# Float32 down products, without parts, in three of seven blocks of the wide experts

## The chip, the cores and the metric

The kernel runs on one core of a Trainium2 chip. The metric is device time in microseconds (us), the median of several executions; lower is better. TensorE is called PE here (its weight loads PEld), VectorE DVE, ScalarE ACT, GpSimd POOL and SyncE SP, as in the profile.

## The reference, cut to what matters

A two-layer trunk on 256 tokens of width 1024. Layer 0 is a retention mixer and a dense SwiGLU, layer 1 a pooling mixer and a top-2-of-8 expert SwiGLU. The change lies in the experts:

```python
def _swiglu(h, w_gate, w_up, w_down):
    return (jax.nn.silu(h @ w_gate) * (h @ w_up)) @ w_down

def expert_block(args):
    xblk, e = args
    return _swiglu(xblk, w_gate[e], w_up[e], w_down[e])
```

An expert has three matrices: gate and up, 1024 x 3584 each, and down, 3584 x 1024. All is float32, and so is the output.

## The kernel before, in words

**Precision by parts.** A float32 weight tile is not multiplied as it is loaded. `split` (L113) makes two tiles of type float32r from it: ACT copies it to the high part `w_hi`, and DVE subtracts that from the tile, which leaves the low part `w_lo`. A product of two float32 numbers is then three float32r matmuls (`mm3`: high x high, high x low, low x high), L156 to L158.

**Weights.** `weights` (L136) loads a 128x4096 piece in two tiles of 128x2048 (1 MB each) called `raw`, and splits each. The loads are issued by SP alone, in the order of the program, into a ring of buffers; twelve of them stay in use through the whole expert stage (six `raw`, four `e8`, `cb` and `T_l`), and some others for a few uses at its beginning. `w_hi` and `w_lo` have three buffers of 2048 columns each (`N_SPL`). A `raw` buffer is free again when DVE has written its `w_lo`; the buffers of the parts are free when PE has used them.

**The experts** come in blocks of 512 of the 3584 hidden columns, seven (`NJ`) for each of eight experts, 56 in all. Each block needs a gate, an up and a down piece: six loads, six splits. The three fullest experts after expert 0 are **wide**: they take 128 tokens, and their products are `mm3`, 48 matmuls of 128x512 for gate and up, 24 for down. The others are **narrow**: they take 64 tokens, and the high and low parts of the tokens stand side by side as the 128 stationary columns, so that `mm2` (L738, L739) does with two matmuls what `mm3` does with three: 32 for gate and up, 16 for down, and the halves are added by small matmuls with `fold` (L774). `BLOCKS` sets the order: the seven blocks of expert 0, then seven times the pattern wide, narrow, wide, narrow, wide, narrow, narrow.

**One iteration** of the main loop (L865) does, for block i, the gate products (`pg`), the up products (`pu`), and then the down products of block i-2 (`down_of`). Between them stand small steps: for a wide block `hidden` (ACT: Silu of `pg` into `sg`; DVE: `moe_h` = `pu` times `sg`) and, an iteration later, `moe_T`, which turns the hidden block by four transposes and splits it into `dT`; for a narrow block ACT copies `g_out` and `u_out`, PE folds them, and ACT and DVE make `sg_n`, `h_n` and `dT`. `prepare` and `combine` gather the tokens of the next expert and give back the sums of the last one. `advance` takes the piece that was loaded last and issues the loads and splits of the next. `behind_next` (L823) puts the small steps that it encloses behind the first half of the splits of the piece in `coming`; ACT and DVE run their instructions in the order of the program, so this says where on these engines the small steps stand.

Of the kernel before, what the change touches and what calls it, by code (L numbers as in the profile page):

```python
# [13 lines left out]
AF = mybir.ActivationFunctionType  # L14
# [5 lines left out]
P = 128  # L20
# [11 lines left out]
NJ = DFE // 512  # L32
# [18 lines left out]
WIDE = tuple(0 < p <= N_WIDE for p in range(NE))  # L51

_wide = iter([(p, j) for p in range(1, N_WIDE + 1) for j in range(NJ)])
_narrow = iter([(p, j) for p in range(N_WIDE + 1, NE) for j in range(NJ)])
BLOCKS = [(0, j) for j in range(NJ)] + [next(_wide if t % 7 in (0, 2, 4) else _narrow) for t in range(7 * NJ)]
assert len(set(BLOCKS)) == NE * NJ and BLOCKS[-1] == (NE - 1, NJ - 1)
ALWAYS = math.inf

# [6 lines left out]
def trunk(ctx, tc, x, cols, c_row, const, ada_0, ada, w_0, w_in, w_out, f_gu, f_dn, pool_w, m_g, m_u, m_d, out):  # L65
    nc = tc.nc
# [6 lines left out]
    def bank():  # L73
        return psA.tile([P, 512], F, tag="a", name="bank")

    def tbank():
        return psT.tile([P, 512], F, tag="t", name="tbank")

    def buf(tag, shape, bufs=1, dt=F, name=None):
        return act.tile([P] + shape, dt, tag=tag, name=name or tag, bufs=bufs)  # L80

    def w2(shape, name, dt=F):
        return buf("w2", shape, 4, dt, name)
# [23 lines left out]
    for h in range(2):  # L107
        ps = tbank()
# [3 lines left out]
    def split(hi, lo, src):  # L112
        return nc.scalar.activation(hi, src, AF.Copy), nc.vector.tensor_sub(lo, src, hi.bitcast(F))  # L113

    @contextmanager
    def behind(*instructions):

        with ExitStack() as s:
            for i in instructions:
                s.enter_context(tc.issue_after(i.ins))  # L120
            yield
# [4 lines left out]
    def load(src, in_halves=False):  # L126
        tag, bufs, uses = ring.popleft()
        if uses > 1:
            ring.append((tag, bufs, uses - 1))
        t = buf(tag, [2048], bufs, name="raw")  # L130
        n = 1024 if in_halves else 2048
        for c in range(0, 2048, n):
            nc.sync.dma_start(t[:, c:c + n], src[:, c:c + n])
        return t

    def weights(src, step=2048, held=((), (), (), ()), in_halves=False):  # L136

        parts, splits = [], []
        for h in range(0, src.shape[1], 2048):
            t = load(src[:, h:h + 2048], in_halves)  # L140
            hi = buf("w_hi", [2048], N_SPL, R)
            lo = buf("w_lo", [2048], N_SPL, R)
            for c in range(0, 2048, step):
                strip = slice(c, c + step)
                with behind(*held[len(splits)]):
                    splits.append(split(hi[:, strip], lo[:, strip], t[:, strip]))
            parts.append((hi, lo))

        def at(c, n=512):
            hi, lo = parts[c // 2048]  # L150
            return hi[:, c % 2048:c % 2048 + n], lo[:, c % 2048:c % 2048 + n]
        at.splits = splits
        return at

    def mm3(ps, xh, xl, wh, wl, start, stop):
# [91 lines left out]
    def transpose4(src):  # L247
        ps = tbank()
        for i in range(4):
            nc.tensor.transpose(ps[:, i * P:(i + 1) * P], src[:, i * P:(i + 1) * P], ident)  # L250
        return ps
# [14 lines left out]
    for b in range(TB):  # L266
        for g in range(0, KD, 4):
            ps = transpose4(xn[:, b, g * P:(g + 4) * P])
# [3 lines left out]
    first = [[tbank() for _ in range(TB)]] + [[bank() for _ in range(TB)] for _ in range(3)]  # L272
    for k in range(KD):
# [5 lines left out]
        at = weights(w_0[k], 1024, held=((), h_k))  # L279
# [90 lines left out]
    for i, f in enumerate(W_REST):  # L370
        at = weights(w_in[i])
# [11 lines left out]
    for h in range(NH):  # L383
        yT = st[f"yT{h}"]
        at = weights(w_out[h])
        last = h == NH - 1
# [16 lines left out]
    for b in range(TB):  # L403
# [9 lines left out]
        for g in range(0, KD, 4):  # L413
            ps = transpose4(xn[:, b, g * P:(g + 4) * P])
# [14 lines left out]
    def gu_block(j, hd_before):  # L429
        at = weights(f_gu[j], **{} if j else dict(step=1024, held=(early, early, late, late)))  # L430
        hd = w2([TB, 256], "ffn_h")
        pss = [bank() for _ in range(TB)]
        th = None
        steps = [(b, k) for b in range(TB) for k in range(KD)] if j == 0 else [(b, k) for k in range(KD) for b in range(TB)]
        for i, (b, k) in enumerate(steps):
            if i == 8 and j:
                th = ffn_T(hd_before)
            wh, wl = at(512 * k)
            mm3(pss[b], hh[:, k, tok(b)], hl[:, k, tok(b)], wh, wl, k == 0, k == KD - 1)
        for b in range(TB):  # L440
            sg = w2([256], "sg")
            nc.scalar.activation(sg, pss[b][:, 0:256], AF.Silu)
            nc.vector.tensor_mul(hd[:, b], pss[b][:, 256:512], sg)
        return hd, th

    def down_weights(j):
        return weights(f_dn[:, 2048 * j:2048 * (j + 1)])
# [6 lines left out]
    hd = None  # L454
    for j in range(NFB):
        hd, th = gu_block(j, hd)
        if 0 < j < NFB - 1:
            at = down_weights(j - 1)
# [14 lines left out]
        if j == 9:  # L473
# [6 lines left out]
            ps = tbank()  # L480
            for k in range(KD):
                nc.tensor.matmul(ps[:, 0:NE], s_m[:, k:k + 1].to_broadcast([P, P]), rt0[:, k],
                                 start=(k == 0), stop=(k == KD - 1))
# [3 lines left out]
    last = [(NFB - 2, down_weights(NFB - 2), th)]  # L487
# [37 lines left out]
    for b in range(TB):  # L525
        pooled = [bank() for _ in range(2)]
        for g in range(0, KD, 4):
            ps = transpose4(xn[:, b, g * P:(g + 4) * P])
# [6 lines left out]
        for n in range(2):  # L535
            ps = bank()
# [6 lines left out]
        for n in range(2):  # L543
            band(pooled[n], n, slice(b * P, (b + 1) * P), hw[:, b], b == 0, True)
            c = slice(512 * n, 512 * (n + 1))
# [6 lines left out]
    for b in range(TB):  # L552
        rs.append(normed(xn, b)[2])
        ps = tbank()
# [4 lines left out]
        ps = tbank()  # L559
# [22 lines left out]
    def sources():  # L582

        def rows(a, i):
            p, j = BLOCKS[i]
            if p == 0:
                return a[j * P:(j + 1) * P, :]
            if expert[p] is None:
                expert[p] = nc.values_load(place_i[0:1, p - 1:p], engines=[SP], min_val=1, max_val=NE - 1,
                                           skip_runtime_bounds_check_because="a permutation of 1 to 7")  # L590
            return a[ds((expert[p] * NJ + j) * P, P), :]

        for i in range(n_blocks + 2):
            if i < n_blocks:
                yield rows(m_g, i)
                yield rows(m_u, i)
            if i > 1:
                yield rows(m_d, i - 2)

    srcs = sources()  # L600


# [3 lines left out]
        ring.insert(place, tuple(spare))  # L606
    ring.extendleft(reversed(once))
    with behind(chain_end):
        coming = weights(next(srcs), 1024)

    ps = tbank()
    wh, _ = coming(0)
# [4 lines left out]
    ps = tbank()  # L617
# [137 lines left out]
        nc.vector.tensor_mul(hd, pu, sg)  # L755
        return hd

    def moe_T(hd):
        ps = transpose4(hd)
        th = buf("dT", [2, 4, P], 2, R, name="dT")  # L760
        split(th[:, 0], th[:, 1], ps.rearrange("p (c t) -> p c t", c=4))
        return th
# [6 lines left out]
    def fold_T(gu):  # L769

        ps = tbank().rearrange("p (g c t) -> p g c t", g=2, c=4)
        for i, a in enumerate(gu):
            for c in range(4):
                nc.tensor.matmul(ps[:, i, c], a[:, c * P:(c + 1) * P], fold, start=True, stop=True)  # L774
        sg = w2([4, HALF], "sg_n")
        nc.scalar.activation(sg, ps[:, 0], AF.Silu)
        hd = w2([4, HALF], "h_n")
        nc.vector.tensor_mul(hd, ps[:, 1], sg)
        th = buf("dT", [4, 2, HALF], 2, R, name="dT")
        split(th[:, :, 0], th[:, :, 1], hd)  # L780
        return th

    def down(at, th, ye, first, last, narrow=False):
        for c in range(4):
            for n in range(2):
                wh, wl = at(1024 * c + 512 * n)
                if narrow:
                    mm2(ye[n], th[:, c], wh, wl, first and c == 0, last and c == 3)
                else:
                    mm3(ye[n], th[:, 0, c], th[:, 1, c], wh, wl, first and c == 0, last and c == 3)  # L790
# [31 lines left out]

    def behind_next():  # L823

        return behind(*coming.splits[len(coming.splits) // 2]) if coming else nullcontext()

    def advance():
        nonlocal coming
        at, src = coming, next(srcs, None)
        coming = None if src is None else weights(src)  # L830
        return at

    steps, first_steps = [], []
# [3 lines left out]
            (first_steps or steps).pop(0)()  # L837

    def turned_of(i, parts):
        return moe_T(parts) if WIDE[BLOCKS[i][0]] else fold_T(parts)  # L840

    def picked(a, placed, p):
        return pick(a, 0) if p == 0 else pick(placed, p - 1)
# [1 line left out]
    outs, ths = {}, {}  # L845

    def down_of(i):
        p, j = BLOCKS[i]
        if j == 0:
            outs[p] = [bank(), bank()]  # L850
        down(advance(), ths.pop(i), outs[p], j == 0, j == NJ - 1, not WIDE[p])
        if j == NJ - 1 and p < NE - 1:
            while steps:
                steps.pop(0)()
            steps.extend(combine(outs[p], ready[p][1], picked(gate, gate_p, p), g2_row))
            steps.pop(0)()
# [7 lines left out]
    mid = None  # L864
    for i, (p, j) in enumerate(BLOCKS):  # L865
        wide = WIDE[p]
# [29 lines left out]
    last = coming  # L896
# [21 lines left out]
    with tc.If(most > 0):  # L918
        slot2 = cst.tile([P, TB, NE], F, name="slot2")
        nc.vector.tensor_sub(slot2, slot, room.rearrange("p (o e) -> p o e", o=1).to_broadcast([P, TB, NE]))  # L920
        with tc.For_i(0, NE, 1) as e:
# [10 lines left out]
            ye = [bank(), bank()]  # L932
            for j in range(NJ):
                at = ds((e * NJ + j) * P, P)
                hd = hidden(up(weights(m_g[at, :]), xe), up(weights(m_u[at, :]), xe))
# [87 lines left out]
```

## Time and profile before

| | us |
|---|---|
| median of 3 runs | 1374.58 (1373.06 to 1376.11) |
| the profiled execution, its own time | 1376.74 |
| its span, first to last instruction | 1375.0 |
| PE busy in the span | 1315.1 (96%) |
| PEld busy | 1052.5 (77%) |
| DVE busy | 1215.2 (88%) |
| ACT busy | 978.2 (71%) |
| DMA of the span | 477.30 MB, mean 347 GB/s |

A row of the view of groups gives line, engine, operation, output<-inputs and count, then the busy time and the mean of one. In the view in order of time a row gives start, duration, engine, line and operation, and in brackets how long the engine was idle before it and which instruction ended that. A PE matmul's duration contains its way through the array, in which the next one already runs: what it costs a stream is the distance from its start to the next start.

### The profile page before, as it was taken

What the parts mean: (1) busy time and instruction counts of PE and PEld (TensorE: products, weight loads), DVE (VectorE), ACT (ScalarE), POOL (GpSimd) and SP (SyncE); (2) the same over time, 40 slices, a digit from 0 to 9 for tenths busy, and PEclk for the clock granted to TensorE, in tenths of its full rate; (3) what the DMA queues carried; (4) which work ended last, traced back from release to release, by engine and by line L of the source; (5) the groups of instructions that cost most, each with busy time, mean ns of one, the idle gap of its engine ahead of it and who ended that gap; (6) DMA issues with size and microseconds to landing.
All of it is one profiled execution on the core that took longest, in us unless ns stands there. A gap on an engine that the chain in (4) does not pass through costs nothing.

```text
span 1375.0 us, 16794 instructions
## 1 busy us (share of the span) xinstructions
PE 1315.1 (96%) x6136; PEld 1052.5 (77%) x6136; DVE 1215.2 (88%) x1121; ACT 978.2 (71%) x942; POOL 0.2 (0%) x4
## 2 busy tenths in 40 slices
PE   7999998999999899999999999999999999999995
PEld 5787876888887777778778877788778777777874
DVE  7889867998867698999989999989998989999997
ACT  6655465444445698878878887878878878788884
POOL 0000000000000000000000000000000000000000
PEclk9999999999999899999999999999999999999998
DMA  9987885998786599999999999999999999999960
GB/s 384 380 278 260 324 287 207 338 378 362 297 333 238 209 427 344 369 364 424 419 377 401 424 334 334 412 356 426 412 357 409 360 334 401 404 367 418 424 279 33
DMA packets 66474, 477.30 MB, mean 347 GB/s; under 512 B 7377, under 2 KB 7761, under 8 KB 8658
## 3 DMA queue, kind: packets, MB, share of 16 engines
q1 hardware_dynamic: 66386, 476.17, 88.3%
q8 instruction: 50, 0.82, 0.2%
q14 instruction: 38, 0.31, 0.1%
HBM read 475.10 MB, written 1.05 MB: 346 GB/s over the span
## 4 chain that ended last, share of the span: by engine, by line
PE 70%; DVE 16%; ACT 6%; issue 4%; DMA 3%; DVEq 0%; SPq 0%; ACTq 0%
PE bank L157 15%; PE bank L158 15%; PE bank L156 14%; DVE w_lo L113 12%; PE bank L739 8%; PE bank L738 7%; PE tbank L774 3%; ACT w_hi L113 3%; DMA raw<-in_m_d_dram 2%; PE tbank L720 2%; PE tbank L250 1%; DVE raw L167 1%; ACT xe_f L240 1%; DMA raw<-in_m_u_dram 1%; DVE dT L113 1%
## 5 line engine op out<-in xcount | busy, mean ns | idle before, releaser
L113 DVE TENSOR_TENSOR w_lo<-raw,w_hi 128x2048 fp32r<-128x2048 f32 (+1 forms) x413 | 907.1, 2225 | 82.5 <-ACT w_hi L113 78.4
L113 ACT ACTIVATE w_hi<-raw 128x2048 fp32r<-128x2048 f32 (+1 forms) x413 | 763.8, 1868 | 199.1 <-PE bank L158 142.3
L739 PE MATMUL bank<-w_lo,xe_n 128*128 128x512 f32 x560 | 230.7, 412 | 12.7 <-DVE w_lo L113 9.6
L738 PE MATMUL bank<-w_hi,xe_n 128*128 128x512 f32 x560 | 221.1, 396 | 2.0 <-DVE xe_n L113 2.0
L739 PEld LDWEIGHTS bank<-w_lo,xe_n 128*128 128x128 f32 x560 | 105.8, 189 | 57.5 <-DVE w_lo L113 38.0
L156 PE MATMUL bank<-w_hi,T_h 128*128 128x512 f32 x352 | 140.9, 401 | 3.0 <-ACT T_h L113 3.0
L157 PE MATMUL bank<-w_lo,T_h 128*128 128x512 f32 x352 | 138.5, 393 | 2.4 <-DVE w_lo L113 2.4
L158 PE MATMUL bank<-w_hi,T_l 128*128 128x512 f32 x352 | 138.8, 394 | 1.7 <-DVE T_l L113 1.7
L157 PE MATMUL bank<-w_lo,xe 128*128 128x512 f32 x336 | 132.5, 394 | 0.9 <-DVE w_lo L113 0.9
L156 PE MATMUL bank<-w_hi,xe 128*128 128x512 f32 x336 | 131.6, 392 | 0.0
L158 PE MATMUL bank<-w_hi,xe 128*128 128x512 f32 x336 | 130.9, 390 | 0.0
L738 PEld LDWEIGHTS bank<-w_hi,xe_n 128*128 128x128 f32 x560 | 106.0, 189 | 22.1 <-DVE xe_n L113 2.1
L167 DVE SCALAR_TENSOR_TENSOR raw<-raw,cb 128x1024 f32<-128x1024 f32 x96 | 114.4, 1218 | 1.7 <-DMA raw<-in_ada_dram 1.7
L739 PE MATMUL bank<-w_lo,dT 128*128 128x512 f32 x280 | 104.4, 411 | 7.2 <-DVE w_lo L113 6.7
L738 PE MATMUL bank<-w_hi,dT 128*128 128x512 f32 x280 | 100.1, 394 | 1.7 <-DVE dT L113 1.7
L157 PE MATMUL bank<-w_lo,dT 128*128 128x512 f32 x256 | 100.8, 394 | 0.7 <-DVE w_lo L113 0.7
L158 PE MATMUL bank<-w_hi,dT 128*128 128x512 f32 x256 | 99.8, 390 | 0.0
L156 PE MATMUL bank<-w_hi,dT 128*128 128x512 f32 x256 | 94.2, 389 | 0.0
L156 PEld LDWEIGHTS bank<-w_hi,T_h 128*128 128x128 f32 x352 | 66.6, 189 | 17.7 <-ACT T_h L113 4.3
L158 PEld LDWEIGHTS bank<-w_hi,T_l 128*128 128x128 f32 x352 | 66.5, 189 | 17.1 <-DVE T_l L113 3.2
L157 PEld LDWEIGHTS bank<-w_lo,T_h 128*128 128x128 f32 x352 | 66.6, 189 | 16.4 <-DVE w_lo L113 2.8
L157 PEld LDWEIGHTS bank<-w_lo,xe 128*128 128x128 f32 x336 | 63.1, 188 | 16.3 <-DVE w_lo L113 3.8
(227 smaller groups left out, 1430.5 us busy)
## 6 DMA issues: line engine op xcount, KB each, us to landing
raw<-in_m_g_dram SPq DMA_DIRECT2D x112, 1024.0 KB, 7.5
raw<-in_m_u_dram SPq DMA_DIRECT2D x112, 1024.0 KB, 7.6
raw<-in_m_d_dram SPq DMA_DIRECT2D x112, 1024.0 KB, 7.3
raw<-in_ada_dram SPq DMA_DIRECT2D x48, 1024.0 KB, 7.2
raw<-in_f_gu_dram SPq DMA_DIRECT2D x22, 1024.0 KB, 6.9
raw<-in_w_in_dram SPq DMA_DIRECT2D x16, 1024.0 KB, 5.2
raw<-in_f_dn_dram SPq DMA_DIRECT2D x11, 1024.0 KB, 7.2
raw<-in_w_dram SPq DMA_DIRECT2D x8, 1024.0 KB, 8.7
```

Source lines behind the costliest of these rows:

```text
L113: return nc.scalar.activation(hi, src, AF.Copy), nc.vector.tensor_sub(lo, src, hi.bitcast(F))
L156: nc.tensor.matmul(ps, xh, wh, start=start, stop=False)
L157: nc.tensor.matmul(ps, xh, wl, start=False, stop=False)
L158: nc.tensor.matmul(ps, xl, wh, start=False, stop=stop)
L167: nc.vector.scalar_tensor_tensor(s, s, 1.0, cb, op0=ALU.mult, op1=ALU.mult, accum_out=mod[:, m:m + 1])
L240: nc.scalar.activation(out, ps, AF.Identity, scale=a[:, k:k + 1], bias=s[:, k:k + 1])
L250: nc.tensor.transpose(ps[:, i * P:(i + 1) * P], src[:, i * P:(i + 1) * P], ident)
L720: nc.tensor.matmul(ps[:, i * ns:(i + 1) * ns], xn[:, b, c], oh[:, b, 0:ns], start=(b == 0), stop=(b == TB - 1))
L738: nc.tensor.matmul(ps, x, wh, start=start, stop=False)
L739: nc.tensor.matmul(ps, x, wl, start=False, stop=stop)
L774: nc.tensor.matmul(ps[:, i, c], a[:, c * P:(c + 1) * P], fold, start=True, stop=True)
```

## The change

In the blocks 1, 3 and 5 (of 0 to 6) of each wide expert, nine blocks in all, the down piece is loaded and not split. `moe_T` then makes one float32 tile (`dT_f`, by one ACT copy) in place of the two parts, and `down` does eight float32 matmuls of 128x512 on the `raw` tiles in place of 24 float32r ones. `behind_next` has nothing to stand behind where such a piece is in `coming`.

```diff
+WHOLE = {(p, j) for p, j in BLOCKS if WIDE[p] and j % 2}
...
+    def whole_weights(src):
+
+        parts = [load(src[:, h:h + 2048]) for h in range(0, src.shape[1], 2048)]
+
+        def at(c, n=512):
+            return parts[c // 2048][:, c % 2048:c % 2048 + n]
+        at.splits = []
         return at
...
-                yield rows(m_g, i)
-                yield rows(m_u, i)
+                yield weights, rows(m_g, i)
+                yield weights, rows(m_u, i)
             if i > 1:
-                yield rows(m_d, i - 2)
+                yield whole_weights if BLOCKS[i - 2] in WHOLE else weights, rows(m_d, i - 2)
...
-    def moe_T(hd):
+    def moe_T(hd, whole=False):
         ps = transpose4(hd)
+        if whole:
+            t = buf("dT", [4, P], 2, name="dT_f")
+            nc.scalar.activation(t, ps.rearrange("p (c t) -> p c t", c=4), AF.Copy)
+            return t
...
-    def down(at, th, ye, first, last, narrow=False):
+    def down(at, th, ye, first, last, narrow=False, whole=False):
         for c in range(4):
             for n in range(2):
+                if whole:
+                    nc.tensor.matmul(ye[n], th[:, c], at(1024 * c + 512 * n), start=first and c == 0, stop=last and c == 3)
+                    continue
...
-        return behind(*coming.splits[len(coming.splits) // 2]) if coming else nullcontext()
+        return behind(*coming.splits[len(coming.splits) // 2]) if coming and coming.splits else nullcontext()
```

**What moves on DVE.** The place is the iteration of a wide block after a narrow one, whose down piece is a whole one (the fourth wide place of the second wide expert). Before, from the `moe_h` of the wide block ahead of it:

```order
578 L755 TENSOR_TENSOR moe_h<-bank,sg 128x512
579 L113 TENSOR_TENSOR w_lo<-raw,w_hi 128x2048 x4
580 L113 TENSOR_TENSOR dT<-tbank,dT 128x512
581 L113 TENSOR_TENSOR w_lo<-raw,w_hi 128x2048 x6
582 L778 TENSOR_TENSOR h_n<-tbank,sg_n 128x256
583 L113 TENSOR_TENSOR w_lo<-raw,w_hi 128x2048
584 L113 TENSOR_TENSOR dT<-h_n,dT 128x4x64
585 L113 TENSOR_TENSOR w_lo<-raw,w_hi 128x2048
586 L755 TENSOR_TENSOR moe_h<-bank,sg 128x512
587 L113 TENSOR_TENSOR w_lo<-raw,w_hi 128x2048 x4
```

Now:

```order
564 L766 TENSOR_TENSOR moe_h<-bank,sg 128x512
565 L115 TENSOR_TENSOR w_lo<-raw,w_hi 128x2048 x10
566 L793 TENSOR_TENSOR h_n<-tbank,sg_n 128x256
567 L115 TENSOR_TENSOR dT<-h_n,dT 128x4x64
568 L766 TENSOR_TENSOR moe_h<-bank,sg 128x512
569 L115 TENSOR_TENSOR w_lo<-raw,w_hi 128x2048 x4
```

The subtraction for `dT` of the whole block and the two splits of its down piece are gone; `moe_h`, which needs the up products of this iteration, now follows `dT` directly.

**What moves on ACT.** The place is the last narrow block of the first pattern that has a whole down piece in its iteration. Before:

```order
361 L113 ACTIVATE w_hi<-raw 128x2048 x4
362 L766 ACTIVATE g_out<-bank 128x512
363 L776 ACTIVATE sg_n<-tbank 128x256
364 L113 ACTIVATE w_hi<-raw 128x2048
365 L113 ACTIVATE dT<-h_n 128x4x64
366 L113 ACTIVATE w_hi<-raw 128x2048
367 L766 ACTIVATE u_out<-bank 128x512
368 L113 ACTIVATE w_hi<-raw 128x2048 x4
```

Now:

```order
357 L115 ACTIVATE w_hi<-raw 128x2048 x4
358 L781 ACTIVATE g_out<-bank 128x512
359 L791 ACTIVATE sg_n<-tbank 128x256
360 L115 ACTIVATE dT<-h_n 128x4x64
361 L781 ACTIVATE u_out<-bank 128x512
362 L115 ACTIVATE w_hi<-raw 128x2048 x4
```

The two copies of the down piece are gone, and `u_out`, which needs the up products, stands ahead of the four copies of the next gate and up pieces with only `dT` before it. On SP nothing moves.

## Rows read from the trace of the kernel before

**Rows 1.** The page: busy time of each engine over the span.
```profile
PE 1315.1 (96%) x6136; PEld 1052.5 (77%) x6136; DVE 1215.2 (88%) x1121; ACT 978.2 (71%) x942; POOL 0.2 (0%) x4
```

**Rows 2.** Busy by stretch: expert stage; a narrow and a wide iteration (with PEclk, DMA share, GB/s).
```profile
475.00:1345.00 870.00, 845.69 (x4011) 678.09 (x4010) 814.75 (x509) 720.20 (x591) 0.00 (x0) 1.00 0.96 381
946.90:960.30 13.40, 13.39 (x65) 10.54 (x64) 12.98 (x8) 12.55 (x10) 0.00 (x0) 1.00 1.01 426
960.30:977.10 16.80, 16.80 (x78) 13.91 (x77) 15.84 (x10) 12.82 (x10) 0.00 (x0) 1.00 1.01 426
```

**Rows 3.** The page: the chain of waits over the span, by engine.
```profile
PE 70%; DVE 16%; ACT 6%; issue 4%; DMA 3%; DVEq 0%; SPq 0%; ACTq 0%
```

**Rows 4.** In order of time: PE through a wide block's down products, 24 matmuls.
```profile
970.51 0.62 PE L156 MATMUL bank<-w_hi,dT 128*128 128x512 f32 x2
...
975.73 0.39 PE L158 MATMUL bank<-w_hi,dT 128*128 128x512 f32 x1
975.96 0.39 PE L738 MATMUL bank<-w_hi,xe_n 128*128 128x512 f32 x1
```

**Rows 5.** In order of time, PE: two float32 matmuls of 128x512 (L340) and the next.
```profile
81.57 1.88 PE L340 MATMUL bank<-a,sT 128*128 128x512 f32 x4
83.29 1.02 PE L342 MATMUL bank<-a,sT 128*128 128x512 f32 x2
```

**Rows 6.** Float32 matmuls at the kernel's end (L807): all of them; weight loads in time.
```profile
L807 PE MATMUL tbank<-yp,ohT x8: 592/592/697, 1359.7 to 1363.2; 128*128 128x512 f32 x8
...
1360.26 0.19 PEld L807 LDWEIGHTS tbank<-yp,ohT 128*128 128x128 f32 x1 [0.24 <-issue]
1360.69 0.19 PEld L807 LDWEIGHTS tbank<-yp,ohT 128*128 128x128 f32 x1 [0.24 <-issue]
```

**Rows 7.** Instructions by tile, 475 to 1345 us: ns min/median/max; loads from issue to landing.
```profile
L113 DVE TENSOR_TENSOR w_lo<-raw,w_hi x326: 2278/2286/2296, 473.0 to 1342.7; 128x2048 fp32r<-128x2048 f32 x163
L113 ACT ACTIVATE w_hi<-raw x325: 1892/1919/1993, 477.1 to 1342.9; 128x2048 fp32r<-128x2048 f32 x163
L113 DVE TENSOR_TENSOR dT<-tbank,dT x21: 682/684/687, 580.8 to 1323.7; 128x512 fp32r<-128x512 f32 x21
DMA to landing us min/median/max: 4.7/7.4/10.2
```

**Rows 8.** Waits of PE and of PEld, 475 to 1345 us: total, times, longest.
```profile
PE bank L739 <- DVE w_lo L113: 16.3, 29, 1.4
PE bank L157 <- DVE w_lo L113: 1.6, 5, 0.5
PEld bank L739 <- DVE w_lo L113: 57.1, 98, 1.9
PEld bank L157 <- DVE w_lo L113: 5.8, 14, 1.0
```

**Rows 9.** Waits of PEld: first and last of nine stretches, 623.2 to 668.8 and 1301.5 to 1331.7.
```profile
PEld bank L739 <- DVE w_lo L113: 2.1, 5, 0.5
...
PEld bank L739 <- DVE w_lo L113: 1.1, 3, 0.4
```

**Rows 10.** In order of time, ACT in the wide iteration of rows 2.
```profile
962.55 1.92 ACT L113 ACTIVATE w_hi<-raw 128x2048 fp32r<-128x2048 f32 x1 [1.12 <-PE bank L158]
965.27 1.92 ACT L113 ACTIVATE w_hi<-raw 128x2048 fp32r<-128x2048 f32 x1 [0.53 <-PE bank L158]
```

**Rows 11.** In order of time, ACT, DVE and PE in the narrow iteration after it.
```profile
980.28 0.60 ACT L766 ACTIVATE g_out<-bank 128x512 f32<-128x512 f32 x1
980.77 0.59 ACT L113 ACTIVATE dT<-tbank 128x512 fp32r<-128x512 f32 x1
981.25 3.73 ACT L113 ACTIVATE w_hi<-raw 128x2048 fp32r<-128x2048 f32 x2
...
983.21 6.70 DVE L113 TENSOR_TENSOR w_lo<-raw,w_hi 128x2048 fp32r<-128x2048 f32 x3
...
985.55 0.73 PE L739 MATMUL bank<-w_lo,dT 128*128 128x512 f32 x2 [0.56 <-DVE w_lo L113]
```

**Rows 12.** In order of time, SP: loads into freed buffers around that down piece's splits.
```profile
969.55 3.10 SPq L133 DMA_DIRECT2D raw<-in_m_d_dram  x2
975.12 2.92 SPq L133 DMA_DIRECT2D raw<-in_m_g_dram  x2
```

More of the change, by code (lines that the diff above doesn't have):

```diff
@@ L152, in weights @@
         at.splits = splits
+        return at
+    def whole_weights(src):
[3 more added lines that the diff above has]
+        at.splits = []
         return at
@@ L608, in trunk @@
     with behind(chain_end):
-        coming = weights(next(srcs), 1024)
+        coming = weights(next(srcs)[1], 1024)
     ps = tbank()
@@ L823, in behind_next @@
     def behind_next():
-        return behind(*coming.splits[len(coming.splits) // 2]) if coming else nullcontext()
+        return behind(*coming.splits[len(coming.splits) // 2]) if coming and coming.splits else nullcontext()
     def advance():
         nonlocal coming
-        at, src = coming, next(srcs, None)
-        coming = None if src is None else weights(src)
+        at = coming
+        take, src = next(srcs, (None, None))
+        coming = take and take(src)
         return at
@@ L839, in turned_of @@
     def turned_of(i, parts):
-        return moe_T(parts) if WIDE[BLOCKS[i][0]] else fold_T(parts)
+        return moe_T(parts, BLOCKS[i] in WHOLE) if WIDE[BLOCKS[i][0]] else fold_T(parts)
     def picked(a, placed, p):
@@ L850, in down_of @@
             outs[p] = [bank(), bank()]
-        down(advance(), ths.pop(i), outs[p], j == 0, j == NJ - 1, not WIDE[p])
+        down(advance(), ths.pop(i), outs[p], j == 0, j == NJ - 1, not WIDE[p], BLOCKS[i] in WHOLE)
         if j == NJ - 1 and p < NE - 1:
```

## The prediction

> **What bounds the kernel now.** I read the page's busy times first, then the chain of waits, then the stretches of the expert stage, then single iterations in order of time. The page has PE at 96% and DVE at 88% [rows 1], and PE carries 70% of the chain, DVE 16% [rows 3]. Between 475 and 1345 us, where all of the change lies, PE is busy 845.69 us of 870, DVE 814.75 and ACT 720.20 [rows 2]: two engines near their limit, so averages do not decide. Single iterations do. In a wide iteration PE is busy 16.80 of 16.80 us and DVE 15.84; ACT there stands idle until PE gives a part's buffer back (1.12 and 0.53 us) [rows 2, 10]. So wide iterations are PE's. In a narrow iteration DVE has 12.98 of 13.40 us, PE waits for `w_lo` now and then [rows 2, 11], and these iterations are shared between DVE and the way from PE over ACT and DVE back to PE. The change takes work from DVE and ACT and gives some to PE, and six of its nine down products stand in wide iterations, three in the last narrow one of a pattern.
>
> **The change part by part.**
>
> *PE, down products.* Before, a wide down takes from 970.51 to 975.96 us, 5.45 us for 24 matmuls, 0.227 each [rows 4]. A float32 matmul of 128x512 stands in the trace as two records: `give` issues four of them at the end, and there are eight [rows 6]. Two of them in `attend` take from 81.57 to 83.29 us, 0.43 per record, and the weight loads of the last ones follow each other in 0.43 too [rows 5, 6]. Eight whole products are then 16 x 0.43 = 6.88 us. That is 1.43 us more per block, 12.9 us over nine. PE's stream is closed in these iterations, so I take all of it as time. Both costs are seen in this trace, and I give them no range.
>
> *DVE.* Nine blocks lose two `w_lo` of 2.286 us and one `dT` subtraction of 0.684: 9 x 5.26 = 47.3 us [rows 7]. *ACT* loses two `w_hi` of 1.919 us each, 34.5 us [rows 7]; the copy to `dT_f` costs what the copy to `dT` did. These are worth only what PE waits for them.
>
> *What PE can win back.* Over the whole stage PE idles 16.3 + 1.6 = 17.9 us for `w_lo`, and its weight loads wait 57.1 + 5.8 = 62.9 us for it, mostly while a matmul still runs [rows 8]. The relief is local: with three buffers of parts, DVE and ACT can be ahead by three tiles and no more. I asked for these waits in the nine stretches that hold an iteration with a whole down and the narrow or short ones that follow it. The weight loads wait there 2.1, 1.0, 1.1, 2.6, 6.2, 1.3, 3.1, 2.4 and 1.1 us, 20.9 in all (the first and the last stand in [rows 9]); PE itself idles in about a quarter of that, as in the whole stage (17.9 of 62.9 [rows 8]), about 6 us. So the gain lies between 0 and 20.9 us. I take 4.5, near PE's own waits, since those are time and a weight load that waits behind a running matmul is not; and not all 6, for this reason: in the narrow iteration after a whole down, `w_lo` of the down piece is late because ACT takes `g_out` when the gate products end (980.28), then `dT`, and only then the two `w_hi` (981.25), DVE follows at 983.21, and PE gets its operand at 985.55 [rows 11]. The order of ACT is unchanged there, the start is set by PE, and DVE's reserve shortens none of it.
>
> *Waits that the change adds.* `moe_h` (DVE) and `u_out` (ACT) now reach the head of their queues early and wait for the up products, with the next gate piece's splits behind them. PE does 6.88 us of whole products meanwhile, or what is left of them where the scheduler puts one or two ahead. DVE needs 0.684 + 2.286 us from the end of `pu` to the first `w_lo`, about 3.0, and 5.3 to the second; in the narrow case ACT needs 0.60 for `u_out` and 1.92 for `w_hi`, and DVE 2.29, about 4.8 [rows 7, 10, 11]. Both are under 6.88, or 5.2 with two products ahead, so I cost them at nothing. Where the gathers of `prepare` stand behind `u_out` the cover is thin: bounds 0 and 2.5 us in each of the three narrow places, taken as 0, the 7.5 kept for the upper end.
>
> *DMA.* The loads of the whole tiles give their buffers back when PE has read them: the first about half of the down products after `pu`, the second at their end. Before, DVE freed them so that SP issued the next loads from 969.55 on [rows 12]; with `pu` ending about 970.5 [rows 4], that is now about 974 and 977.4, some 4 to 5 us later for two loads, and the next are back in step. Twelve buffers at six tiles per iteration cover two iterations, 13.40 + 16.80 = 30.2 us, of which a load takes 7.4 from issue to landing [rows 2, 7]: some 20 us of reserve, so I cost it at nothing.
>
> *Sum.* +12.9 - 4.5 = +8.4 us. On the profiled execution's 1376.74 that gives 1385.1. It lies 2.2 us above the median, so for the median of 1374.58 I predict 1383.0 us, 0.6% slower.
>
> **Rule against row.** In the wide iteration PE starts a matmul each 0.227 us [rows 4], and PEld is busy 13.91 of 16.80 us, 83% [rows 2]. One load of 0.19 us [rows 6] per 0.227 is just that share, so 83% is what a closed stream of these shapes shows, and the stage's 678.09 of 870, 78%, is 94% of it. The Trainium skill (Perfetto Trace Analysis, Identifying the Most-Contended Engine) holds matmul occupancy to be a poor measure of TensorE's headroom and judges by the busy share of weight loads instead. By that reading TensorE would have over a fifth to spare, DVE at 94% would be the bound, and the 47.3 us would come off: about 1327. The trace agrees that PE's busy time overstates it, but the spacing of the starts shows no room in the wide iterations.
>
> **The rivals.**
>
> *DVE is the bound after all: faster.* For it: DVE's 12.98 of 13.40 us in narrow iterations, and waits for `w_lo` of 62.9 us in the stage [rows 2, 8]. The place is the narrow iterations after a whole down; the mechanism is DVE's reserve of three tiles, carried on. It decides the sign once it recovers more than 12.9 us. With all 20.9 us the sum is -8.0 and the time 1366.6; the rule's 47.3 would be its far end. Against it: the chain over ACT, and ACT's idle time for PE's buffers [rows 10, 11]. Chance 0.11. With it goes the case that the product is not what the records say, one pass in place of four (8 x 0.227 = 1.8 us per block, -32.7 us in all, about 1342): the eight records for four instructions speak against it. Chance 0.01.
>
> *The two cancel: no change.* The recovered waits come to between 10 and 15.6 us, half to three quarters of the 20.9. Time 1372 to 1377, centre 1374.6. Chance 0.20.
>
> *The buffers held longer starve the loads: slower still.* The steady iterations already load at 426 GB/s [rows 2], so lost transfer time comes back slowly. If each pair of late loads costs 2.4 us in the end (4.4 to 5 late, less what is queued), 9 x 2.4 = 21.6 us come on top: about 1404. It decides from the point where the reserve of some 20 us is used up. The thin cover of the gathers (7.5 us, 1390.5) goes here too. Chance 0.08.
>
> **How the numbers follow.** The forecast, 1377.3 to 1390 with 1383.0 as its centre, has 0.60. A measurement of this kernel can tell about 0.2%, 2.75 us, from no change: faster is below 1371.8, slower above 1377.3. Faster 0.12 (first rival with its side case), same 0.20, slower 0.60 + 0.08 = 0.68. The range, 1372 to 1390, leaves out the 0.12 below and 0.08 above; its upper end is the cost of 12.9 with nothing won back and one thin cover paid.
>
> **What would show it.** Right: the float32 records of the down products start 0.43 us apart, a wide iteration with a whole down is 18.2 us long where 16.8 stood, the narrow one after it stays above 12.9, DVE's busy time falls by about 47 us and ACT's by 34, and ACT and DVE show new idle time before `moe_h` and `u_out`. Wrong: narrow iterations after a whole down near 12.4 us; PE's waits for `w_lo` in the stage far under 10 us; waits of PE or ACT for `raw` loads; a spacing other than 0.43.

## The result and the profile after

The changed kernel takes 1386.72 us (median of 4 runs, 1386.29 to 1389.43) where the kernel before took 1375.34 beside it (4 runs, 1373.06 to 1377.25). The ratio is 1.0088, 95% interval [1.0067, 1.0108]: slower by 0.9%, some 12 us. The two profiled spans, 1387.6 and 1375.0 us, differ by 12.6.

The page of the kernel after, busy time by engine, which answers to [rows 1]:

```profile
PE 1325.9 (96%) x6064; PEld 1040.4 (75%) x6064; DVE 1170.8 (84%) x1094; ACT 944.1 (68%) x924; POOL 0.2 (0%) x4
```

DVE lost 44.4 us and ACT 34.1. PE has 72 matmul records less (nine times 24 became 16) and is busy 10.8 us longer.

The float32 products of the nine blocks, by tile (nanoseconds as minimum, median, maximum; then first and last start):

```profile
L802 PE MATMUL bank<-raw,dT_f x144: 590/592/648, 633.3 to 1329.2; 128*128 128x512 f32 x144
```

There are 144 records for 72 matmuls, two for each. How far apart they start stands in PE's and PEld's rows in order of time, in the same wide iteration as [rows 4]:

```profile
972.49 1.02 PE L802 MATMUL bank<-raw,dT_f 128*128 128x512 f32 x2
...
975.66 0.39 PE L169 MATMUL bank<-w_hi,xe 128*128 128x512 f32 x1
975.88 6.17 PE L802 MATMUL bank<-raw,dT_f 128*128 128x512 f32 x14
...
976.32 0.19 PEld L802 LDWEIGHTS bank<-raw,dT_f 128*128 128x128 f32 x1 [0.24 <-issue]
...
981.03 0.19 PEld L802 LDWEIGHTS bank<-raw,dT_f 128*128 128x128 f32 x1 [0.24 <-issue]
```

From the weight load at 976.32 to the one at 981.03 there are eleven steps, 4.71 us, 0.428 each. Two records stand ahead of the last up products, fourteen behind them. A whole down is 16 x 0.428 = 6.85 us where 24 x 0.227 = 5.45 stood: 1.40 more, and nine times that is 12.6, the whole difference of the spans. That is a match of sums. Counted from first gate product to first gate product, the iteration with the whole down and the next one together take 0.9 to 1.5 us more in seven of the nine places; in the other two, where gathers moved into the iteration ahead, the three iterations take 0.6 and 2.4 more.

Two iterations in a row (wide with a whole down; narrow after it), each from its fourth gate product to that of the next: busy time of PE, PEld, DVE, ACT, POOL, then granted clock, DMA share and GB/s:

```profile
964.70:982.90 18.20, 18.20 (x68) 12.32 (x67) 13.69 (x9) 9.90 (x8) 0.00 (x0) 1.00 0.87 349
982.90:996.50 13.60, 12.28 (x51) 8.79 (x50) 10.71 (x8) 10.71 (x9) 0.00 (x0) 1.00 1.00 399
```

The same narrow iteration in the kernel before:

```profile
977.10:990.50 13.40, 12.35 (x49) 8.61 (x48) 12.97 (x9) 11.67 (x9) 0.00 (x0) 1.00 1.02 405
```

The wide one grew from 16.80 [rows 2] to 18.20 and PE has no gap in it. DVE has 4.5 us to spare there now, and the narrow iteration behind it is no shorter, although DVE is busy only 10.71 us of it where it was 12.97.

PE's waits and PEld's waits over the expert stage (475 to 1357 us: total, times, longest), which answer to [rows 8]:

```profile
PE bank L750 <- DVE w_lo L115: 18.6, 35, 1.4
...
PE bank L168 <- DVE w_lo L115: 1.4, 4, 0.5
...
PEld bank L750 <- DVE w_lo L115: 54.9, 88, 1.9
...
PEld bank L168 <- DVE w_lo L115: 5.4, 13, 1.0
```

PE waits 20.0 us for `w_lo` where it waited 17.9, and its weight loads 60.3 where they waited 62.9. With 44 us less to do, DVE delivers no earlier.

Why not, is in ACT's, DVE's and PE's rows from the end of the up products of that wide iteration on:

```profile
976.13 1.91 ACT L115 ACTIVATE w_hi<-raw 128x2048 fp32r<-128x2048 f32 x1 [0.47 <-ACT w_hi L115]
984.04 1.92 ACT L115 ACTIVATE w_hi<-raw 128x2048 fp32r<-128x2048 f32 x1 [6.00 <-PE bank L749]
986.23 0.60 ACT L781 ACTIVATE g_out<-bank 128x512 f32<-128x512 f32 x1 [0.28 <-PE bank L750]
986.73 0.59 ACT L115 ACTIVATE dT<-tbank 128x512 fp32r<-128x512 f32 x1
987.20 3.72 ACT L115 ACTIVATE w_hi<-raw 128x2048 fp32r<-128x2048 f32 x2
...
976.08 0.69 DVE L766 TENSOR_TENSOR moe_h<-bank,sg 128x512 f32<-128x512 f32 x1 [3.57 <-PE bank L169]
976.69 6.69 DVE L115 TENSOR_TENSOR w_lo<-raw,w_hi 128x2048 fp32r<-128x2048 f32 x3
985.99 2.29 DVE L115 TENSOR_TENSOR w_lo<-raw,w_hi 128x2048 fp32r<-128x2048 f32 x1 [2.61 <-ACT w_hi L115]
...
989.15 6.70 DVE L115 TENSOR_TENSOR w_lo<-raw,w_hi 128x2048 fp32r<-128x2048 f32 x3 [0.27 <-ACT w_hi L115]
...
991.50 0.73 PE L750 MATMUL bank<-w_lo,dT 128*128 128x512 f32 x2 [0.82 <-DVE w_lo L115]
```

DVE waits 3.57 us for the up products, then makes three `w_lo` while PE does the whole products. ACT meanwhile stands 6.00 us until PE frees a buffer of parts. The narrow iteration then runs as before: `g_out` starts when the gate products end (986.23), `dT` follows, then the down piece's `w_hi` (987.20), its `w_lo` (989.15), and PE goes on at 991.50. From `g_out` to PE that is 5.27 us. In [rows 11] it is 985.55 - 980.28 = 5.27 too. PE's wait at its end is 0.82 where 0.56 stood.

SP's rows around the whole piece:

```profile
978.65 3.77 SPq L135 DMA_DIRECT2D raw<-in_m_d_dram  x2
982.68 0.94 SPq L135 DMA_DIRECT2D raw<-in_m_g_dram  x2
```

The two buffers of the whole piece come free 2.8 and 6.8 us after the up products (975.9). The iteration's DMA share falls to 0.87 and is 1.00 in the next; no wait of PE for a load stands in the list of its waits.

### The profile page after: what moved, and what is told of

It reads as the page before. It is cut to its first block, busy times and chain, and to the rows that moved or that the text cites. A ratio compares the mean times of both kernels' runs of the same rounds, so it can differ in the third digit from the quotient of the medians.

```text
span 1387.6 us, 16560 instructions
## 1 busy us (share of the span) xinstructions
PE 1325.9 (96%) x6064; PEld 1040.4 (75%) x6064; DVE 1170.8 (84%) x1094; ACT 944.1 (68%) x924; POOL 0.2 (0%) x4
## 5 line engine op out<-in xcount | busy, mean ns | idle before, releaser
L115 DVE TENSOR_TENSOR w_lo<-raw,w_hi 128x2048 fp32r<-128x2048 f32 (+1 forms) x395 | 865.8, 2222 | 113.5 <-ACT w_hi L115 108.5
L115 ACT ACTIVATE w_hi<-raw 128x2048 fp32r<-128x2048 f32 (+1 forms) x395 | 728.3, 1865 | 220.3 <-PE bank L169 144.8
L750 PE MATMUL bank<-w_lo,dT 128*128 128x512 f32 x280 | 104.1, 411 | 8.0 <-DVE w_lo L115 7.5
L749 PE MATMUL bank<-w_hi,dT 128*128 128x512 f32 x280 | 99.9, 394 | 1.7 <-DVE dT L115 1.7
L167 PEld LDWEIGHTS bank<-w_hi,T_h 128*128 128x128 f32 x352 | 66.6, 190 | 17.9 <-ACT T_h L115 4.4
L167 PEld LDWEIGHTS bank<-w_hi,xe 128*128 128x128 f32 x336 | 63.1, 188 | 14.2 <-issue 0.5
L169 PEld LDWEIGHTS bank<-w_hi,xe 128*128 128x128 f32 x336 | 63.1, 188 | 13.6 <-issue 1.0
L168 PE MATMUL bank<-w_lo,dT 128*128 128x512 f32 x184 | 72.3, 393 | 0.5 <-DVE w_lo L115 0.5
```

The lines of the kernel that those rows point to most:

```text
L167: nc.tensor.matmul(ps, xh, wh, start=start, stop=False)
L168: nc.tensor.matmul(ps, xh, wl, start=False, stop=False)
L169: nc.tensor.matmul(ps, xl, wh, start=False, stop=stop)
L749: nc.tensor.matmul(ps, x, wh, start=start, stop=False)
L750: nc.tensor.matmul(ps, x, wl, start=False, stop=stop)
```

## The experiments

The theory after the result: **PE pays 1.40 us for each whole down, and the time taken off DVE and ACT is worth nothing**, because ACT's order and PE's buffers set when `w_lo` comes. The rivals: DVE's relief does pay and something else costs as much; or it is held up by the three buffers of parts and would pay with more; or it pays in another order of ACT's work.

**The products alone, the splits kept.** The down pieces are loaded, split and multiplied as float32; nobody reads the parts.

```diff
...
-        parts = [load(src[:, h:h + 2048]) for h in range(0, src.shape[1], 2048)]
+        raws = []
+        w = weights(src, raws=raws)
...
-        at.splits = []
+        at.splits = w.splits
```

> The float32 down products of the change stay, but their down pieces are split as before and the parts are not read: PE pays the whole price, DVE and ACT get no relief, and the small steps stand where they stood before. Theory (the nine float32 downs cost 1.4 us of PE each, and the relief of DVE and ACT is worth nothing, since their reserve is capped by three buffers of parts): within 3 us of the change, 10 to 14 us above the kernel before. Rival (the relief does win time back, 4.5 us or more): 4.5 us or more above the change, 16 or more above before.

Measured: 1387.16 us (6 runs) beside 1374.97; ratio 1.0087 [1.0071, 1.0103]. That is the change's own 1.0088. PE's waits in the stage (475 to 1357 us):

```profile
PE bank L753 <- DVE w_lo L115: 17.6, 33, 1.4
PE bank L171 <- DVE w_lo L115: 1.4, 4, 0.5
```

With DVE and ACT doing nearly all of their old work (1210.2 and 976.4 us on the page) the waits and the time are the same. The theory held. The total alone leaves the first rival open: this run takes away the change's new waits together with its relief, and the two could cancel. The two iterations (wide with a whole down, narrow after it, columns as above) tell more:

```profile
964.70:982.80 18.10, 18.10 (x68) 12.32 (x67) 16.72 (x11) 13.55 (x10) 0.00 (x0) 1.00 0.87 352
982.80:996.40 13.60, 12.27 (x51) 8.78 (x50) 12.11 (x8) 10.70 (x9) 0.00 (x0) 1.00 0.99 394
```

DVE is busy 3.0 and 1.4 us longer in them than in the change, and they are as long to 0.1 us. `g_out` starts at 986.14 and PE goes on with `w_lo` at 991.41, 5.27 us later once more. In seven of the nine places the gate, the up and the down stretch of both iterations each agree with the change to 0.05 us; in the other two, gathers lie in another iteration. So in these seven neither the relief nor the new waits move PE, and the rival that one pays for the other falls there.

**The relief alone, first form.** The nine pieces are loaded but not split, and PE does 24 float32r matmuls per down on a small constant tile, 32 columns repeated 16 times.

```diff
...
+    fixed = fix.rearrange("p (o c) -> p o c", o=1).to_broadcast([P, 16, 32])
...
+                    mm3(ye[n], th[:, 0, c], th[:, 1, c], fixed, fixed, first and c == 0, last and c == 3)
```

> The nine down pieces are loaded and not split, as in the change, but their products are 24 float32r matmuls of 128x512 as before, on a constant tile in place of the weights (the down weights of these nine blocks are left out of the result). PE pays what it paid before, DVE and ACT have the full relief of 47 and 34 us less the 6 us of the dT parts, and the loaded buffers are free at once. Theory: 0 to 4 us below the kernel before. Rival (the relief is worth time, and late free buffers or new waits of ACT and DVE took it back in the change): 5 to 20 us below before.

Measured: 1404.9 us, ratio 1.0214 [1.0199, 1.0229]. Neither theory said so, and the run tells nothing of the relief, for its PE order is another one. PE in order of time:

```profile
972.44 0.40 PE L172 MATMUL bank<-fix,dT 128*128 128x512 f32 x1
...
973.86 0.40 PE L172 MATMUL bank<-fix,dT 128*128 128x512 f32 x1
```

These stand among the up products, ahead of where a real down product can stand, since they depend on no piece, and leave the place behind the up products with less work in it. They also start 0.237 us apart (972.44 to 973.86, six steps), not 0.227. And the granted clock of TensorE was at the lower of its two levels (1.2 GHz, not 2.4) in four stretches of the expert stage, 24 us in all; the kernel before has none there. One of them begins at 905 us: from 900 to 910 PE was busy 5.57 us and the mean granted clock 0.75. Half of the 24 us, 12 of the 30 us lost, is an estimate of the most that this can have cost. What each of the three costs was not measured.

**The relief alone, second form.** The same with the down products held behind the last up product, and with a plain tile of 512 token columns as their operand.

```diff
...
+                    w = xe_n[:, state[1], 0:4].rearrange("p k a b -> p (k a b)")
+                    mm3(ye[n], th[:, 0, c], th[:, 1, c], w, w, first and c == 0, last and c == 3)
...
+        with behind(state[0]) if BLOCKS[i] in WHOLE else nullcontext():
+            down(advance(), ths.pop(i), outs[p], j == 0, j == NJ - 1, not WIDE[p], BLOCKS[i] in WHOLE)
```

> As the run of the relief alone, with two repairs: the nine down products are held behind the last up product on PE, as they stand before, so that the scheduler can't put them far ahead of their place; and their moving operand is a float32r tile of the tokens, 512 columns in a row, in place of the constant of 32 repeated columns. The down weights of these nine blocks are left out of the result. PE pays what it paid before, DVE and ACT have the relief. Theory (relief worth nothing): within 3 us of the kernel before. Rival (relief worth time, taken back in the change by late buffers or new waits): 5 to 20 us below before.

Measured: 1375.47 us (12 runs) beside 1375.27; ratio 0.9996 [0.9988, 1.0005]. The same two iterations, wide with such a down and narrow after it (columns as above):

```profile
959.60:976.40 16.80, 16.80 (x78) 13.92 (x77) 13.22 (x9) 10.00 (x8) 0.00 (x0) 1.00 1.01 428
976.40:989.80 13.40, 12.06 (x49) 8.67 (x48) 11.11 (x7) 10.70 (x8) 0.00 (x0) 1.00 1.02 418
```

DVE and ACT are relieved as in the change, PE's time is the old one, and the iterations are 16.80 and 13.40 as before. The relief alone, with the new waits of `moe_h` and `u_out` still in it, is worth 0.5 us with an interval from -0.7 to 1.7. In the seven places the two iterations together agree with the kernel before to 0.05 us; in the two where gathers moved, -0.8 and +0.9 us cancel. The theory held.

**One pass in place of three.** As the second form, with one of the three products.

```diff
-                    mm3(ye[n], th[:, 0, c], th[:, 1, c], w, w, first and c == 0, last and c == 3)
+                    nc.tensor.matmul(ye[n], th[:, 0, c], w, start=first and c == 0, stop=last and c == 3)
```

> As the run before it, with one pass in place of three: eight float32r matmuls per down (two of the three products and the weights are left out of the result), 1.8 us of PE where 5.45 stood. Theory (in these iterations time follows PE's work and nothing else): 9 x 3.6 = 33 us off in the most, 20 to 33 us below the kernel before, as DVE or the chain over ACT becomes the bound of an iteration somewhere on the way. Rival (DVE or the chain sets these iterations already): under 12 us below before.

Measured: 1360.19 us, ratio 0.989 [0.9872, 0.9908], 15.1 us under the kernel before. It lies between the two expectations. PE's own saving is 16 x 0.227 = 3.6 us per block, 32.7 in all; half of it was lost. The rows of DVE and PE in order of time at such a place:

```profile
962.57 0.69 DVE L769 TENSOR_TENSOR moe_h<-bank,sg 128x512 f32<-128x512 f32 x1 [2.67 <-PE bank L169]
963.18 6.69 DVE L115 TENSOR_TENSOR w_lo<-raw,w_hi 128x2048 fp32r<-128x2048 f32 x3
...
962.37 1.98 PE L802 MATMUL bank<-xe_n,dT 128*128 128x512 f32 x8
...
965.51 0.50 PE L750 MATMUL bank<-w_lo,xe_n 128*128 128x512 f32 x1 [0.50 <-DVE w_lo L115]
```

PE's waits in the stage (475 to 1340 us) are 28.0 us where they were 17.9:

```profile
PE bank L750 <- DVE w_lo L115: 21.2, 38, 1.8
PE bank L168 <- DVE w_lo L115: 6.8, 7, 1.8
```

`moe_h` stands ahead of the gate piece's `w_lo` and waits for the up products. The first `w_lo` is ready at 965.47, 2.9 us after `moe_h` starts. Eight short products and the transposes (962.37 to 964.54) cover that no longer, and PE waits. In the change 6.85 us of float32 products do. So the new wait that the prediction costed at nothing is real, and free only behind products that are long enough. That these waits make up all of the missing 17.6 us is not shown.

**Four buffers of parts.** Both kernels with two `raw` buffers less and one pair of parts more.

```diff
-N_RAW, N_SPL, N_E8, N_OHT = 6, 3, 4, 4
+N_RAW, N_SPL, N_E8, N_OHT = 4, 4, 4, 4
```

> The change with four buffers of parts in place of three, and four raw buffers of the first kind in place of six, so that the memory is the same (two loads less of reserve). Theory (three buffers cap the reserve of DVE and ACT): 6 to 15 us below the change, and nearer than 12 us to the kernel before with the same four buffers, since now part of the relief reaches PE. Rival (the order of ACT in narrow iterations alone sets the late parts): within 3 us of the change.

> The kernel before with four buffers of parts and four raw buffers. Theory: 3 to 10 us below the kernel before, since DVE, at 94% in the stage, gains a tile of reserve through the wide iterations. Rival (order of ACT alone): within 3 us of before. If the loads run short with two buffers less, it is slower, and ACT shows waits for raw tiles.

Measured: the change 1383.87 us, ratio 1.0065 [1.0051, 1.0078]; the kernel before 1371.78, ratio 0.9976 [0.9968, 0.9985]. Both gain some 3 us, and the distance between them stays at 12.1. For the change 6 to 15 us were expected by the theory, so it failed there; for the kernel before the gain lies on the border of the two expectations. A fourth buffer gives the relieved engines nothing that it doesn't give the others, so the three buffers are not what makes the relief worthless (with four `raw` buffers; more parts beside six `raw` were not tried).

**Another order on ACT and DVE.** Four buffers of parts, and the loads and splits of the next piece are issued ahead of the small steps, which then stand behind the down piece's first split. `behind_next` takes the number of that split.

```diff
...
-        with behind_next():
+        at_u = advance()
+        with behind_next(0):
...
-        pu = up(advance(), ready[p][0], not wide)
+        pu = up(at_u, ready[p][0], not wide)
```

The kernel before, and then the change:

> The kernel before with four buffers of parts and four raw buffers (as in the run of that name), and one move: the down piece is taken before the small steps between gate and up products, and these steps (g_out, the turning of the block before) stand behind its first split in place of the second split of the up piece. Theory (in narrow iterations the late low part of the down piece comes from ACT's order, g_out and dT ahead of its copy): the waits of PE for w_lo in down products fall to under half, 5 to 15 us below the same kernel without the move. Rival (DVE's whole load sets the narrow iterations): within 2 us of it.

> The change with the same four buffers and the same move. Theory (PE's price is fixed; the relief of DVE is worth something only where the order of ACT lets it through): 4 to 12 us above the run before it. Rival (the relief is worth nothing in any order): 12 us or more above it. A third way: below it, if DVE is the bound once the chain over ACT is gone.

Measured: the kernel before in this order 1354.62 us (4 runs, 1353.51 to 1358.26), ratio 0.9854 [0.9835, 0.9872]. That is 17.2 under the same kernel in the old order with four buffers, where 5 to 15 were expected, and the fastest of all kernels run. ACT, DVE and PE, in order of time, in the iteration that answers to [rows 11]:

```profile
960.57 3.98 ACT L113 ACTIVATE w_hi<-raw 128x2048 fp32r<-128x2048 f32 x2 [0.75 <-PE bank L158]
964.69 0.60 ACT L766 ACTIVATE g_out<-bank 128x512 f32<-128x512 f32 x1
965.19 0.60 ACT L113 ACTIVATE dT<-tbank 128x512 fp32r<-128x512 f32 x1
965.66 1.92 ACT L113 ACTIVATE w_hi<-raw 128x2048 fp32r<-128x2048 f32 x1
...
967.62 2.29 DVE L113 TENSOR_TENSOR w_lo<-raw,w_hi 128x2048 fp32r<-128x2048 f32 x1
...
968.12 0.62 PE L738 MATMUL bank<-w_hi,dT 128*128 128x512 f32 x2
968.57 0.62 PE L739 MATMUL bank<-w_lo,dT 128*128 128x512 f32 x2
```

The busy times of that iteration, columns as above:

```profile
961.70:973.90 12.20, 11.23 (x49) 8.93 (x48) 11.33 (x8) 10.03 (x9) 0.00 (x0) 1.00 1.01 423
```

Only one `w_hi` of the down piece is left behind `g_out` and `dT`; the other was made ahead of them. PE goes into the down products without a wait, and the iteration takes 12.20 us where 13.40 stood (13.42 with four buffers in the old order), with more work on DVE than in the change. PE's idle time for `w_lo` ahead of the narrow down products (L739 with `dT`) fell from 10.3 us to 3.9. So it was the order of the small steps and the splits that made `w_lo` late. That ACT's part of it decides is read from [rows 11], where the first `w_hi` starts at 981.25 and `w_lo` at 983.21, one `w_hi` of 1.92 us later; DVE's order changed too, and no run parts the two. The loads are the same, so their DMA share of 0.96 in the stage [rows 2] did not bound the kernel before either.

The change in this order took 1372.81 us (12 runs), ratio 0.998 [0.997, 0.999], 18.2 above its partner. Expected were 4 to 12 if the relief pays once the order allows it. It doesn't pay here either; the distance is even 5.6 above PE's 12.6.

**The small steps in that order.** Where a whole piece comes there is no split of it to stand behind, and the small steps stand ahead of the up piece's splits. Here they are put behind its second split.

```diff
...
-        with behind_next(0):
+        with behind_next(0) if coming and coming.splits else behind(*at_u.splits[1]):
```

> The changed kernel with four parts and the down piece's first split ahead of the small steps, and where the piece that comes is a whole one (no split to stand behind) the small steps stand behind the up piece's second split. Theory: of the 18.2 us by which the changed form lies above the form with split parts in this order, 12.6 are PE's float32 records (9 x 1.40) and the other 5.6 the place of the small steps, so 12 to 14 us above e8_before_down_split_first, about 1367 to 1369. Rival: the 5.6 us is not in the place of the small steps; then it stays 17 to 19 above, about 1372 to 1373.

Measured: 1368.44 us (4 runs) beside 1376.36, ratio 0.9938 [0.9919, 0.9957]. Each against the kernel before that ran beside it, it lies 12.7 us above the split form (-7.9 and -20.7), give or take 3.7 by the two intervals. The wide iteration with a whole down, with the steps ahead (the run before):

```profile
954.70:972.60 17.90, 17.70 (x66) 11.80 (x64) 12.39 (x8) 12.73 (x9) 0.00 (x0) 1.00 0.87 349
```

The same with the steps behind:

```profile
952.40:969.80 17.40, 17.40 (x64) 11.85 (x63) 12.21 (x9) 11.05 (x9) 0.00 (x0) 1.00 0.90 365
```

The 5.6 was the place of the small steps, and what is left is, within the noise, PE's price again, 9 x 1.40.

**All 21 wide blocks whole.**

```diff
-WHOLE = {(p, j) for p, j in BLOCKS if WIDE[p] and j % 2}
+WHOLE = {(p, j) for p, j in BLOCKS if WIDE[p]}
```

> The change for all 21 blocks of the wide experts in place of nine. Theory (each whole down costs PE its 1.40 us and the relief of DVE and ACT is worth nothing): 21 x 1.40 = 29 us above the kernel before, 26 to 33, about 1401 to 1408. Rival (with more blocks whole, DVE comes far enough ahead that its relief of 21 x 5.26 = 110 us begins to pay): under 20 us above, below 1395.

Measured: 1402.2 us (4 runs) beside 1376.36, ratio 1.0186 [1.0167, 1.0205], 25.8 us or 1.23 per block, just under the 26 to 33 of the theory and far from under 20. PE's waits for `w_lo` in the stage (475 to 1372 us) are 16.6 us:

```profile
PE bank L750 <- DVE w_lo L115: 15.4, 34, 1.5
...
PE bank L168 <- DVE w_lo L115: 1.2, 3, 0.5
```

One narrow iteration near the stage's beginning, columns as above, in the kernel before:

```profile
609.10:623.20 14.10, 13.43 (x66) 10.91 (x65) 14.10 (x9) 12.58 (x10) 0.00 (x0) 1.00 0.96 353
```

And with all blocks whole:

```profile
609.60:623.10 13.50, 13.50 (x70) 11.06 (x69) 10.58 (x6) 12.01 (x9) 0.00 (x0) 1.00 1.01 428
```

In this place DVE was busy 14.10 us of 14.10 before, full indeed, and the iteration is 0.6 us shorter now. Relief may pay where DVE has no idle time at all; but the whole down just ahead is also longer on PE and gives DVE time, and no run parts the two. All in all, 21 x 5.26 = 110 us taken off DVE go with some 3.6 us less than PE's price (29.4 less 25.8; by the interval 1.2 to 6.4).

## Why the prediction was right or wrong

Slower was right, and so was the reason: PE's stream is closed and a float32 product is longer on it than three float32r ones. Step by step:

- **PE, down products: right.** 6.85 us where 6.88 was worked out from a prologue row [rows 5], +12.6 where +12.9 stood, in the spans and in the run that keeps the splits.
- **DVE and ACT: right.** -44.4 and -34.1 us on the page where 47.3 and 34.5 were expected.
- **What PE can win back: wrong, the term that failed.** The prediction put it at 4.5 us, between bounds of 0 and 20.9, because PE idles for `w_lo` near the whole downs. Measured, it is 0: waits of 20.0 us against 17.9, and the relief alone at 0.9996. The prediction had the reason in hand, the way over `g_out`, `dT` and `w_hi` on ACT, and used it only to shave the term from 6 to 4.5. The rows show it at work in the iteration of [rows 11], 5.27 us with and without the relief, and the other order of ACT and DVE took away most of PE's waits ahead of narrow down products: `w_lo` is late because DVE's input is late. The forecast of +8.4 was off by this term, with 0.3 the other way from the spacing: 12.6 in the spans (11.4 between the medians).
- **The waits that the change adds: right,** and right that they are hidden. `moe_h` waits 3.57 us, and the cover is real: with products 1.8 us long it no longer holds.
- **DMA: right.** The buffers come free 2.8 and 6.8 us after the up products (3.5 and 6.9 were expected), and the loads keep up: ACT's waits for them in the stage are 4.5 us where 14.1 stood.
- **The rival that DVE is the bound: fell.** It asked for more than 12.9 us from the relief. DVE's busy share of 94% in the stage [rows 2] was no bound; a narrow iteration with DVE busy 10.71 us and one with 12.11 both take 13.60 (the change, and the run with the splits kept).
- **Rule against row.** Weight loads fell from 77% of the span to 75% while the kernel became slower. By the Trainium skill (Perfetto Trace Analysis, Identifying the Most-Contended Engine) TensorE would have gained headroom; this case disagrees, since a float32 record holds PE 0.428 us for one weight load of 0.19. The busy share of weight loads compares streams of one kind only.

## What to carry to other kernels

Before time taken off a busy engine is counted as a gain, follow the operand that the bounding engine waits for back through its makers: if the maker starts late because an in-order queue ahead of it holds steps that wait for the bounding engine itself, a faster maker may give nothing, and another order of that queue can give more than the whole exchange (here 17 us for a few lines, against 0 for 44 us less work on DVE). An exchange of work between engines has two sides with a run for each: here one kept the splits and took the products, the other took the relief at PE's old price, and the two add up to the result within the noise. A wait that a change moves to the front of a queue is free only as long as the work that covers it is.

## What the runs showed that was not expected

PE's list of waits shows only part of what late operands cost. From the old order to the new one, both with the kernel before's products and four buffers, the time fell by 17.2 us (19.4 between the two profiled spans, 1371.4 and 1352.0), but PE's waits for `w_lo` only from 19.4 to 15.2. The page of the old order:

```profile
PE 1312.0 (96%) x6136; PEld 1055.9 (77%) x6136; DVE 1209.6 (88%) x1121; ACT 964.2 (70%) x942; POOL 0.2 (0%) x4
```

And of the new:

```profile
PE 1298.1 (96%) x6136; PEld 1056.4 (78%) x6136; DVE 1207.9 (89%) x1121; ACT 969.0 (72%) x942; POOL 0.2 (0%) x4
```

The same 6136 records are 13.9 us shorter in sum. Not all of that is waiting: ahead of the experts the two profiled runs differ in granted clock (0.98 in the old order and 1.00 in the new from 150 to 300 us). From the first block's first gate product to the last block's, PE's 4026 records in both take 842.3 us of 866.7 in the old order and 834.5 of 851.7 in the new: of 15.0 us only 7.3 are idle time less, and 7.7 are busy time less. So part of the waiting is counted as busy PE. The waits of PEld saw it. In the old order (475 to 1345 us):

```profile
PEld bank L739 <- DVE w_lo L113: 51.4, 78, 1.9
PEld bank L157 <- DVE w_lo L113: 6.6, 17, 0.7
```

In the new (475 to 1330 us):

```profile
PEld bank L739 <- DVE w_lo L113: 31.7, 45, 2.0
PEld bank L157 <- DVE w_lo L113: 4.2, 8, 1.4
```

They fell by 22.1. So the prediction's view that a weight load waiting behind a running matmul costs nothing undersells such waits, and a wait for `w_lo` is better read from both lists. The Trainium skill (Perfetto Trace Analysis, Tensor Engine Instruction) says that a matmul's end in the trace is an estimate and not observed; these rows agree with it.

A float32 product of 128x512 costs 2 x 0.428 = 0.857 us, 3.8 times a float32r one (0.227). The Trainium skill (FP8 and Floating Point Precision, TensorE Precision Notes) has four passes for true float32; the trace agrees in size, and shows them as two records. Three float32r products, 0.68 us, are still cheaper for PE, by a fifth.
